# The pointwise product of a convolution branch moves into a recurrent scan, as filler

## The chip, the cores and the metric

The kernel runs on one core of a Trainium2 chip. The time is device microseconds of one execution, start to end, median of several runs. A core has a matrix engine (PE in the profile, whose weight loads are shown apart as PEld), a vector engine (DVE), a scalar engine (ACT), a general engine (POOL), and a queue of commands of its own for each; SP only issues DMAs. Engines run their own instructions in order, and wait for one another through semaphores.

## The reference, cut to what matters

One encoder layer over 1024 positions and 1024 features, all in float32. A combined projection feeds two mixers and two gates; the mixers' outputs are merged, projected, and followed by a feed-forward block.

```python
h = _rmsnorm(x, attn_norm_w)
proj = einsum("bsd,de->bse", h, w_in)             # 1024 -> 8192
glu_in, q, v, z_f, z_b, og, g_a, g_b = split(proj)
a = glu(glu_in)                                   # 512 channels
a = _dwconv_centred(a, dw_w, dw_b)                # 31 taps
a = silu(_layernorm(a, ln_w, ln_b))               # over the 512 channels
a = einsum("bsc,cd->bsd", a, pw_w)                # pointwise product, 512 -> 1024
o = _bi_hgrn2(q, v, z_f, z_b, lb[0], lb[1])       # two gated linear scans, 8 heads of 128
of = rmsnorm_per_head(o) * norm_w
b = einsum("bse,ed->bsd", of * silu(og), o_w)
y = sigmoid(g_a) * a + sigmoid(g_b) * b
x = x + y @ w_out
x = x + (silu(_dwconv3(h2 @ W_gate)) * (h2 @ W_up)) @ W_down,  h2 = _rmsnorm(x)
return _rmsnorm(x, final_norm_w)
```

Of the scan, only what the order of work depends on is needed here: it goes head by head; for each head and each half of the positions the scores inside chunks of 64 are built up by levels (blocks of 8, 16, 32, 64), each level scaling the queries and keys of the next by decays.

## The kernel before, in words

Everything is kept transposed: features in the 128 partitions, positions along the free axis, in two halves of 512. A product of float32 operands is made from three matmuls: `split` (L123) cuts an operand into a high part (a cast on ACT) and a low part (a subtraction on DVE), and `mm3` (L147 to L149) adds high by high, high by low and low by high into one PSUM bank. One such triple is a 128x128 weight block by 512 positions.

The order of PE's instructions is the order in which the program writes them. On the other engines a scheduler orders the instructions, by when it reckons that each can start and by the order in the program.

**Jobs, pieces and streams.** A dense product is a job with two steps: `prep` loads a column block of 128 weights and splits it, `run` issues the matmuls and the evacuation and yields between pieces. A piece of a plain job (`std_job`) is two triples, 6 matmuls; a job over 1024 input features and both halves has 8 pieces, one over 512 features 4. `duo_job` runs two plain jobs side by side, half by half. `pair_job` makes two column blocks with seven products instead of eight block products (a Strassen scheme), with sums of weights and of results made on DVE, ACT and POOL; it has 14 pieces. `run_jobs` strings jobs together, and prepares the next job's weights ahead of its run. A `Stream` hands out pieces: `fill(n)` issues n more of them, fractions being carried over. So a stream of dense work can be laid between the instructions of something else: this is called filler below. `later(n, do)` puts off an action for n pieces.

**Stages.** (1) Up to 84 us: the norm, and the GLU's columns of the projection. (2) 84 to about 430 us: 17 pair jobs make 34 columns of the projection. Beside them `conv_steps` does the depthwise convolution on DVE: 4 channel groups by 31 taps, each tap one operation over 1024 positions (`acc`, L955). After each tap `CONV_FILL` pieces of the pairs are issued. A finished channel group goes to a DRAM scratch, `d_cv`. (3) For each half, the four groups are loaded back (`cx`), summed (`total`, L967), normalised and put through silu, with `LN_FILL` and `LN_LAST` pieces between; their split parts stay in the pages `ch`. (4) The pointwise product: eight plain jobs for each half, over 512 features (4 blocks), with weights `conv_pw_w`, put into the same list as the pairs that are left; results go to the scratch `d_a`. It ends at about 503 us. (5) The scan, until 880 us. `scan_inputs` loads q and the two forget gates (`zi`, L1063) two halves ahead; `Base` makes decays and keys (`Kh`, L1045) and the scores inside blocks of 8 (L1174); `scan_levels` goes through four levels. On each level PE multiplies (`sc`, `ob`: L1162 and L1188), and then DVE scales the keys kG and queries qF by the decays (`tt`, L1042), which the next level's product reads. `scan_states` makes the states of the chunks (transposes `tr`, L1245, and products, L1254) and `outputs` the results of a head (L1295, transposes L1321), stored as `d_bm`. After each level and each step of the states, seven places in a half, stands

```python
def between(fill):
    dense.fill(fill)
    if ahead is not None:
        ahead.step(BASE_STEPS)
    pending.fill(1)
```

where `dense` is the stream of the 22 columns of the projection that the pairs left (the last two as a `duo_job`), `ahead` the next half's `Base`, and `pending` the outputs of the head before. 21 pieces are issued before the first half, `FILL` at each place, and the pieces that are left in the tail, between the outputs of the last head. (6) From 930 us the product with `hgrn_o_w`, whose evacuation `merge` loads `d_a` and the gates; then `w_out` and the feed-forward block, with the same plain and pair jobs.

The activations of the projection stay on chip for half 0 and for a part of half 1; the first blocks of half 1 are loaded and split again for the scan's filler (`h12`, in pages `hx`, of which there are 32, given out in turn). The pages `hx` are also what the results of the scan are loaded into (`bm_loads`).

Of the kernel before, what the change touches and what calls it, by code (L numbers as in the profile page):

```python
# [10 lines left out]
F32 = mybir.dt.float32  # L11
# [5 lines left out]
AX = mybir.AxisListType  # L17

P = 128
FILL = 1.3  # L20
CONV_FILL = 1.6
NPAIRS = 17
LN_FILL = 6
LN_LAST = 12
# [22 lines left out]
def tile_hybrid_encoder(  # L47
# [22 lines left out]
    nc = tc.nc  # L70
    PSUM = bass.MemoryType.PSUM
    V, A, G, T = nc.vector, nc.scalar, nc.gpsimd, nc.tensor

    S, D = x.shape[1], x.shape[2]
    ND = D // P
    CW = conv_dw_w.shape[2]
    CK = conv_dw_w.shape[1]
    NCW = CW // P
# [14 lines left out]
    def nm(s):  # L93
        uid[0] += 1
        return f"{s}_{uid[0]}"
# [3 lines left out]
    def bank(tag):  # L99
        return ps.tile([P, H], F32, tag=tag, name=nm(tag), bufs=BANKS[tag])  # L100

    def page(pool, tag, bufs, dt=F32):
        return pool.tile([P, H], dt, tag=tag, name=nm(tag), bufs=bufs)

    def tmp():
        return page(mp, "tm", 4)

    def ev():
        return page(mp, "ev", 3)

    def hx():
        return page(mp, "hx", 32, F32R)
# [9 lines left out]
    def split(hi, lo, src, eng, late=False):  # L122
        parts = A.copy(hi, src), eng.tensor_tensor(lo, src, hi.bitcast(F32), op=ALU.subtract)  # L123
        if late:
            for i in parts:
                pin(i)
        return hi, lo

    def w_cols(w, r0, nk, c0, cols=P):
        return w[0, r0 : r0 + nk * P, c0 : c0 + cols].rearrange("(k p) e -> p k e", p=P)  # L130

    def raw_w(src, nk):
        t = mp.tile([P, nk, P], F32, tag="wr", name=nm("wr"), bufs=2)
        nc.sync.dma_start(t, src)
        return t

    def w_page(nk, pool=None):
        if pool is None:
            return mp.tile([P, nk, P], F32R, tag="wp", name=nm("wp"), bufs=4)
        return pool.tile([P, nk, P], F32R, tag="wq", name=nm("wq"), bufs=3)  # L140

    def mm3(acc, w, act, k, first, last, again=False):


        whi, wlo = w
        ahi, alo = act
        T.matmul(acc, whi[:, k, :], ahi, start=first, stop=False, skip_group_check=again)  # L147
        T.matmul(acc, whi[:, k, :], alo, start=False, stop=False, skip_group_check=again)  # L148
        T.matmul(acc, wlo[:, k, :], ahi, start=False, stop=last, skip_group_check=again)  # L149
# [7 lines left out]
    def later(n, do):  # L157

        chores.append([n, do])

    def advance_chores(n=1):
        for c in list(chores):
            c[0] -= n
            if c[0] <= 0:
                chores.remove(c)
                c[1]()
# [26 lines left out]
    def run_jobs(jobs, lead=0, prime=0, first=None):  # L193


        live = collections.deque(maxlen=3)

        jobs = jobs if isinstance(jobs, collections.deque) else collections.deque(jobs)
        ready = collections.deque()

        def prepare(n):
            while jobs and len(ready) < n:
                prep, run = jobs.popleft()
                ready.append((run, prep()))
                live.append(ready[-1][1])

        def tick():
            for w in live:
                if isinstance(w, Weights):
                    w.tick()  # L210
            advance_chores()

        prepare(max(prime, 1))
        if prime:
            yield
        while ready:
# [32 lines left out]
    def std_job(src, nk, acts, evac, halves=(0, 1), step=2):  # L249


        def prep():
            raw = raw_w(src, nk)
            return split(w_page(nk), w_page(nk), raw, V)

        def run(w, halves=halves):
            for half in halves:
                acc = bank("mm")
                for k in range(nk):
                    mm3(acc, w, acts(k, half), k, k == 0, k == nk - 1)  # L260
                    if k % step == step - 1 or k == nk - 1:
                        yield
                evac(half, acc)

        return prep, run

    def duo_job(src0, src1, nk, acts, evac0, evac1):

        both = [std_job(src0, nk, acts, evac0), std_job(src1, nk, acts, evac1)]

        def prep():
            return [p() for p, _ in both]

        def run(w):
            for half in range(2):
                for (_, r), wi in zip(both, w):
                    yield from r(wi, (half,))

        return prep, run
# [197 lines left out]
    def scratch(name, *dims):  # L477
        if not dims:
            return dp.tile([P, H], F32, name=name)
        return [scratch(f"{name}_{i}", *dims[1:]) for i in range(dims[0])]  # L480

    d_h = scratch("d_h", ND, 2)
    d_cv = scratch("d_cv", NCW, 2)
    d_a = scratch("d_a", ND, 2)
    d_ga = scratch("d_ga", ND, 2)
    d_gb = scratch("d_gb", ND, 2)
# [12 lines left out]
    def in_cols(c0):  # L499
        return w_cols(w_in, 0, ND, c0)  # L500
# [212 lines left out]
    def store(dst, func=None):  # L713
        def evac(half, x0, x1=None, op=None):
            t = ev()
            if x1 is not None:
                V.tensor_tensor(t, x0, x1, op=op)  # L717
                x0 = t
            if func is not None:
                A.activation(t, x0, func)  # L720
            elif x1 is None:
                A.copy(t, x0)
            nc.sync.dma_start(dst[half], t)

        return evac
# [214 lines left out]
    jobs = collections.deque(in_pair(n) for n in range(1, NPAIRS))  # L940
# [21 lines left out]
    for _ in conv_steps():  # L962
        s_pairs.fill(CONV_FILL)

# [4 lines left out]
            V.tensor_tensor(o, o, t, op=ALU.add)  # L969
        return o  # L970

    pw_jobs = []
    for half in range(2):
        xs = []
        for j in range(NCW):
            if j % 2 == 0:
                both = p1.tile([P, 2, H], F32, tag="ca", name=nm("cx"), bufs=2)
            nc.sync.dma_start(both[:, j % 2, :], d_cv[j][half])
            xs.append(both[:, j % 2, :])
        s_pairs.fill(LN_FILL)  # L980
        mean = bank("ob")
        T.matmul(mean, ones_m, total(xs, tmp()), start=True, stop=True)
        for t in xs:
            V.scalar_tensor_tensor(t, mean, -1.0 / CW, t, op0=ALU.mult, op1=ALU.add)
        s_pairs.fill(LN_FILL)
        sqs = [tmp() for _ in xs]
        for sq, t in zip(sqs, xs):
            A.activation(sq, t, AF.Square)
        rstd = rstd_over_partitions(total(sqs, sqs[0]), CW, "ob", tmp())
        next(rstd)  # L990
        s_pairs.fill(5)
        rs = next(rstd)
        ca = []
        for j, xn in enumerate(xs):
            V.tensor_tensor(xn, xn, rs, op=ALU.mult)
            V.tensor_scalar(xn, xn, vec("lnw", j), vec("lnb", j), op0=ALU.mult, op1=ALU.add)
            A.activation(xn, xn, AF.Silu)
            both = gp0.tile([P, 2, H], F32R, tag="gl", name=nm("ch"), bufs=NCW)
            ca.append(split(both[:, 0, :], both[:, 1, :], xn, V))
        s_pairs.fill(LN_LAST)  # L1000
        at = 0
        while at < len(jobs) and jobs[at] in pw_jobs:
            at += 1
        for i in range(ND):
            job = std_job(
                w_cols(conv_pw_w, 0, NCW, i * P), NCW, lambda k, hf, ca=ca: ca[k], store(d_a[i]), (half,)
            )
            pw_jobs.append(job)
            jobs.insert(at + i, job)
    s_pairs.drain()  # L1010
    Stream(run_jobs(jobs)).drain()
    p1.release()
    gp0.release()

# [1 line left out]
    rest = todo[2 * NPAIRS :]  # L1016
    rest_jobs = [std_job(in_cols(c), ND, h_std, e) for c, e in rest[:-2]]
    (c0, e0), (c1, e1) = rest[-2:]
    rest_jobs.append(duo_job(in_cols(c0), in_cols(c1), ND, h_std, e0, e1))

    h12.clear()
    for k in range(NK2):
# [2 lines left out]
    dense = Stream(run_jobs(rest_jobs))  # L1025
# [343 lines left out]
    for h in range(NH):  # L1369
# [4 lines left out]
        for half in range(2):  # L1374
            i = 2 * h + half
# [12 lines left out]
            for n, _ in enumerate(scan_levels(base, S_t, Tt[:, half])):  # L1388
                if n == 2:
# [4 lines left out]
                    A.copy(v.rearrange("p c e -> p (c e)"), b)  # L1394
                between(FILL)
            qF, kG = base[0], base[1]
            for _ in scan_states(i, kG, v, Tt, Sf, Sb):
                between(FILL)
            kept.append((S_t, v, qF))
            cur = ahead  # L1400
        pending = Stream(outputs(h, kept, Tt, Sf, Sb))

    left = 8 * (len(rest) - 2) + 16 - dense.count
    pending.fill(1)
    dense.fill(left - 20)
    pending.fill(1)
# [209 lines left out]
    gs, jobs = [], []  # L1616
# [183 lines left out]
```

## Time and profile before

| | |
|---|---|
| median of 3 runs | 1791.35 us (1791.15 to 1793.52) |
| span of the profiled execution | 1788.8 us |
| busy PE | 1733.0 us, 97% |
| busy DVE | 1250.4 us, 70% |
| busy ACT | 775.0 us, 43% |
| busy POOL | 153.8 us, 9% |
| moved by DMA | 276.41 MB, mean 155 GB/s |
| HBM read, written | 185.73 MB, 72.61 MB |

The profiled execution is one of its own; the profile gives its span, from the first instruction to the last, and no time from outside, so that its own time is its span and what the device needs around it.

How rows are read: a group of instructions has its line, engine, operation, its output and inputs by the program's names, the number of them, their busy time in us, the mean of one in ns, and the idle time of the engine just before them with what ended it. A row of the waits reads: engine, tile and line that waited, engine, tile and line that released it, us in total, how many, the longest. A row of the timeline reads: start in us, duration, engine, line, operation, and in brackets the idle time before it and its releaser. In a table of stretches each engine has its busy us and, in brackets, its instructions; PEclk is the TensorE clock that was granted, 1 being full speed.

### The profile page before, as it was taken

The page shows a single profiled execution, that of the slowest core. Times are in us where ns is not written, and L with a number is a line of the kernel's source. Part 1 is how long each engine was busy: PE and PEld are TensorE (multiplying, and loading weights), DVE is VectorE, ACT ScalarE, POOL GpSimd, SP SyncE. Part 2 cuts the span into 40 slices and gives each one's busy share as a digit, 9 for nine tenths or more (in the row PEclk, how much of TensorE's full clock was granted, in tenths as well). Part 3 has the DMA queues.
Part 4 walks back from the last instruction along what each step waited for, and adds up shares of the span by engine and source line. Part 5 has one row for each costly group of instructions (what it writes and reads, how often), then busy time and mean ns, then how long its engine had stood idle before and what let it go on. Part 6 is the DMA issues. An engine that isn't in the chain of part 4 may idle for free.

```text
span 1788.8 us, 27583 instructions
## 1 busy us (share of the span) xinstructions
PE 1733.0 (97%) x10632; PEld 1416.7 (79%) x10638; DVE 1250.4 (70%) x1884; ACT 775.0 (43%) x1490; POOL 153.8 (9%) x168
## 2 busy tenths in 40 slices
PE   8989999999999999999999999999999999999997
PEld 6878877888777777777778888878888888888885
DVE  5599999746569999999645557667667667544455
ACT  7344333334555566655442245344344344422123
POOL 2201111000000000000000002011111111000000
PEclk9999999999999999999999999999999999999999
DMA  8657887743663433333257665567667665534233
GB/s 285 216 151 187 185 185 185 199 150 126 199 214 101 125 119 119 119 119 101 90 180 219 200 201 177 153 142 159 151 144 158 142 151 133 161 103 126 79 91 135
DMA packets 317705, 276.41 MB, mean 155 GB/s; under 512 B 14462, under 2 KB 242566, under 8 KB 317574
## 3 DMA queue, kind: packets, MB, share of 16 engines
q1 hardware_dynamic: 276406, 242.15, 43.1%
q0 software_dynamic: 41168, 32.51, 12.6%
q8 instruction: 83, 1.36, 0.3%
q14 instruction: 48, 0.39, 0.1%
HBM read 185.73 MB, written 72.61 MB: 144 GB/s over the span
## 4 chain that ended last, share of the span: by engine, by line
PE 65%; DVE 19%; DMA 5%; issue 4%; ACT 4%; POOL 1%; SPq 0%; POOLq 0%; DVEq 0%; ACTq 0%
PE mm L147 16%; PE mm L148 16%; PE mm L149 16%; PE sc L147 3%; PE sc L149 3%; PE sc L148 3%; DVE acc L955 2%; DVE kG L1042 2%; DVE DE L1042 2%; DVE qF L1042 2%; DVE wp L123 2%; PE tr L147 1%; PE tr L149 1%; PE tr L148 1%; DVE DE L1098 1%
## 5 line engine op out<-in xcount | busy, mean ns | idle before, releaser
L147 PE MATMUL mm<-hx,wp 128*128 128x512 f32 x1128 | 454.8, 403 | 9.8 <-DVE ev L717 4.3
L149 PE MATMUL mm<-hx,wp 128*128 128x512 f32 x1128 | 441.7, 392 | 1.9 <-DVE wp L123 1.9
L148 PE MATMUL mm<-hx,wp 128*128 128x512 f32 x1128 | 441.4, 391 | 0.0
L123 ACT CAST wp<-wr 128x1024 fp32r<-128x1024 f32 (+2 forms) x179 | 167.0, 934 | 359.6 <-PE mm L148 271.5
L147 PEld LDWEIGHTS mm<-hx,wp 128*128 128x128 f32 x1128 | 212.5, 188 | 55.7 <-DVE ev L717 6.7
L123 DVE TENSOR_TENSOR wp<-wr,wp 128x1024 fp32r<-128x1024 f32 (+2 forms) x177 | 191.4, 1082 | 90.4 <-ACT wp L123 90.1
L149 PEld LDWEIGHTS mm<-hx,wp 128*128 128x128 f32 x1128 | 212.6, 188 | 49.3 <-DVE wp L123 3.2
L148 PEld LDWEIGHTS mm<-hx,wp 128*128 128x128 f32 x1128 | 212.9, 189 | 40.4 <-issue 0.2
L955 DVE SCALAR_TENSOR_TENSOR acc<-gl,v_b,acc 128x1024 f32<-128x1024 f32 x120 | 149.0, 1277 | 0.5
L1651 DVE TENSOR_TENSOR xr<-mm,xr 128x512 f32<-128x512 f32 x48 | 33.2, 691 | 73.1 <-PE mm L149 73.1
L367 ACT COPY su<-mm 128x512 f32<-128x512 f32 x78 | 45.2, 579 | 62.5 <-PE mm L149 61.5
L123 ACT CAST wq<-sw 128x1024 fp32r<-128x1024 f32 x39 | 41.0, 1051 | 64.4 <-issue 28.6
L1500 DVE SCALAR_TENSOR_TENSOR tm<-gp,v_a,tm 128x512 f32<-128x512 f32 x88 | 65.9, 749 | 2.0
L147 PE MATMUL mm<-hy,wp 128*128 128x512 f32 x156 | 61.5, 394 | 1.4 <-ACT su L367 1.4
L148 PE MATMUL mm<-hy,wp 128*128 128x512 f32 x156 | 61.1, 392 | 0.0
L147 PE MATMUL sc<-hy,wq 128*128 128x512 f32 x156 | 61.1, 392 | 0.0
L149 PE MATMUL sc<-hy,wq 128*128 128x512 f32 x156 | 61.1, 391 | 0.0
L147 PE MATMUL tr<-hx,wp 128*128 128x512 f32 x156 | 60.8, 390 | 0.0
L149 PE MATMUL tr<-hx,wp 128*128 128x512 f32 x156 | 60.7, 389 | 0.0
L148 PE MATMUL tr<-hx,wp 128*128 128x512 f32 x156 | 60.7, 389 | 0.0
L148 PE MATMUL sc<-hy,wq 128*128 128x512 f32 x156 | 60.7, 389 | 0.0
L149 PE MATMUL mm<-hy,wp 128*128 128x512 f32 x156 | 60.6, 389 | 0.0
(368 smaller groups left out, 3467.6 us busy)
## 6 DMA issues: line engine op xcount, KB each, us to landing
wr<-in_w_in_dram SPq DMA_DIRECT2D x56, 512.0 KB, 4.7
wr<-in_ffn_w_up_dram SPq DMA_DIRECT2D x24, 512.0 KB, 4.9
sw<-in_ffn_w_up_dram SPq DMA_DIRECT2D x44, 256.0 KB, 3.0
d_g<-ft SPq DMA_DIRECT2D x44, 256.0 KB, 2.7
sw<-in_ffn_w_up_dram POOLq DMA_DIRECT2D x20, 512.0 KB, 8.3
sw<-in_w_in_dram SPq DMA_DIRECT2D x34, 256.0 KB, 3.2
d_z<-ev SPq DMA_DIRECT2D x32, 256.0 KB, 3.1
zi<-d_z SPq DMA_DIRECT2D x32, 256.0 KB, 3.2
```

Of the source, the lines that this page charges most:

```text
L123: parts = A.copy(hi, src), eng.tensor_tensor(lo, src, hi.bitcast(F32), op=ALU.subtract)
L147: T.matmul(acc, whi[:, k, :], ahi, start=first, stop=False, skip_group_check=again)
L148: T.matmul(acc, whi[:, k, :], alo, start=False, stop=False, skip_group_check=again)
L149: T.matmul(acc, wlo[:, k, :], ahi, start=False, stop=last, skip_group_check=again)
L367: A.copy(t, acc)
L955: V.scalar_tensor_tensor(acc, g[:, k : k + S], tap(k), acc, op0=ALU.mult, op1=ALU.add)
L1042: V.tensor_tensor(o, a, b, op=op)
L1098: V.reciprocal(ed(D, 7), ed(0, D + 7))
L1500: V.scalar_tensor_tensor(c, g[:, o + k : o + k + H], vec("fdw", k * NF + j), c, op0=ALU.mult, op1=ALU.add,)
L1651: V.tensor_tensor(xr[i][half], acc, xr[i][half], op=ALU.add)
```

## The change

It touches constants and the two places where the pointwise product is made.

- `FILL`, the pieces per place of the scan, goes from 1.3 to 1.58, and `CONV_FILL`, the pieces per tap of the convolution, from 1.6 to 1.4.
- The pointwise jobs are no longer put into the list of pairs. After the layer norm, the split parts of each channel group and half are stored to a new DRAM scratch, `d_ca`: 16 stores of 256 KB. The scan follows the layer norm directly, once the pairs are drained.
- The pointwise product is appended to the filler of the scan, behind the 22 columns: six plain jobs and a duo job, each over both halves, instead of eight jobs for each half. Its matmuls are the same, 192.
- The parts are loaded from `d_ca` into 16 pages `hx`. The loads are put off with `later(8, ...)`: the wait starts when the first pointwise job is prepared, and they are issued eight pieces on, in the middle of the duo job ahead of it. The pages that they take are pages of `h` that the duo job reads last.
- The number of pieces left for the tail is worked out from the longer list.

```diff
-FILL = 1.3
-CONV_FILL = 1.6
+FILL = 1.58
+CONV_FILL = 1.4
...
+    d_ca = scratch("d_ca", NCW, 2, 2)
...
-    pw_jobs = []
     for half in range(2):
...
-        ca = []
         for j, xn in enumerate(xs):
...
             both = gp0.tile([P, 2, H], F32R, tag="gl", name=nm("ch"), bufs=NCW)
-            ca.append(split(both[:, 0, :], both[:, 1, :], xn, V))
+            for dst, part in zip(d_ca[j][half], split(both[:, 0, :], both[:, 1, :], xn, V)):
+                nc.sync.dma_start(dst, part.bitcast(F32))
         s_pairs.fill(LN_LAST)
-        at = 0
-        while at < len(jobs) and jobs[at] in pw_jobs:
-            at += 1
-        for i in range(ND):
-            job = std_job(
-                w_cols(conv_pw_w, 0, NCW, i * P), NCW, lambda k, hf, ca=ca: ca[k], store(d_a[i]), (half,)
-            )
-            pw_jobs.append(job)
-            jobs.insert(at + i, job)
     s_pairs.drain()
-    Stream(run_jobs(jobs)).drain()
...
     rest_jobs.append(duo_job(in_cols(c0), in_cols(c1), ND, h_std, e0, e1))
+    ca = [[None, None] for _ in range(NCW)]
+
+    def ca_loads(half):
+        for j in range(NCW):
+            parts = hx(), hx()
+            for part, src in zip(parts, d_ca[j][half]):
+                nc.sync.dma_start(part.bitcast(F32), src)
+            ca[j][half] = parts
...
+    def pw_first():
+        prep, run = std_job(pw_col(0), NCW, ca_of, store(d_a[0]))
+
+        def loads():
+            later(8, lambda: [ca_loads(half) for half in range(2)])
+            return prep()
+
+        return loads, run
+
+    rest_jobs.append(pw_first())
+    rest_jobs += [std_job(pw_col(i), NCW, ca_of, store(d_a[i])) for i in range(1, ND - 2)]
+    rest_jobs.append(
+        duo_job(pw_col(ND - 2), pw_col(ND - 1), NCW, ca_of, store(d_a[ND - 2]), store(d_a[ND - 1]))
+    )
...
-    left = 8 * (len(rest) - 2) + 16 - dense.count
+    left = 8 * len(rest) + 4 * ND - dense.count
```

Three places of the order show what moves. Names are tiles with a running number. The first is PE's order in the scan, between two products of a level (`tr` is the last transpose of the head before, L1188 the product that reads qF and kG). Before:

```order
L1392 MATMUL tr_6836<-ident,tm_6686 128x128 x4
L147 MATMUL mm_6751<-hx_916,wp_6275 128x512
L148 MATMUL mm_6751<-hx_917,wp_6275 128x512
L149 MATMUL mm_6751<-hx_916,wp_6276 128x512
L147 MATMUL mm_6751<-hx_946,wp_6275 128x512
L148 MATMUL mm_6751<-hx_947,wp_6275 128x512
L149 MATMUL mm_6751<-hx_946,wp_6276 128x512
L1188 MATMUL sc_6814<-qF_6533,kG_6534 64x64 x8
```

and now, in the same place; six more rows like these, with other pages `hx`, stand at the mark, and line numbers are 19 higher in this part:

```order
L1411 MATMUL tr_6628<-ident,tm_6478 128x128 x4
L147 MATMUL mm_6592<-hx_3960,wp_6222 128x512
L148 MATMUL mm_6592<-hx_3961,wp_6222 128x512
L149 MATMUL mm_6592<-hx_3960,wp_6223 128x512
...
L147 MATMUL mm_6592<-hx_905,wp_6222 128x512
L148 MATMUL mm_6592<-hx_906,wp_6222 128x512
L149 MATMUL mm_6592<-hx_905,wp_6223 128x512
L1207 MATMUL sc_6606<-qF_6315,kG_6316 64x64 x8
```

Before, six filler matmuls (a piece) stand ahead of the level's product; now twelve.

The second is DVE's order late in the convolution. `acc` are the taps, of the third and of the last channel group; L967 is the first step of `total` for half 0, which reads the first two channel groups back (`cx`), and so waits for the third group's last tap and a store and a load behind it; `ev` are evacuations of the pairs, and `wp` and `wq` the low parts of their weights. Before:

```order
L123 TENSOR_TENSOR wp_2738<-wr_2731,wp_2737 128x1024
L717 TENSOR_TENSOR ev_2756<-tr_2701,su_2716 128x512
L955 SCALAR_TENSOR_TENSOR acc_2928<-gl_359,v_b,acc_2928 128x1024
L967 TENSOR_TENSOR tm_3497<-cx_3420 128x512
L955 SCALAR_TENSOR_TENSOR acc_2928<-gl_359,v_b,acc_2928 128x1024 x3
L717 TENSOR_TENSOR ev_2803<-su_2788,mm_2700 128x512
```

and now, up to the same evacuation of the same pair:

```order
L968 TENSOR_TENSOR tm_3272<-cx_3222 128x512
L956 SCALAR_TENSOR_TENSOR acc_2760<-gl_375,v_b,acc_2760 128x1024
L718 TENSOR_TENSOR ev_2787<-tr_2728,su_2744 128x512
L123 TENSOR_TENSOR wp_2769<-wr_2762,wp_2768 128x1024
L956 SCALAR_TENSOR_TENSOR acc_2760<-gl_375,v_b,acc_2760 128x1024 x5
L123 TENSOR_TENSOR wq_2777<-sw_2764,wq_2776 128x1024
L718 TENSOR_TENSOR ev_2834<-su_2819,mm_2727 128x512
```

The pair's evacuation in the last row (`ev`, from `su` and `mm`) now comes after 115 taps of the convolution instead of 112.

The third is SP's queue, late in the scan, where there is nothing like it before; `d_bm` are stores of the scan's results, and the five rows between them the first of the 16 loads of the parked parts:

```order
L1346 DMA d_bm_0_273<-ev_8434 128x512
L1016 DMA hx_8616<-d_ca_0_0_119 128x512
L1016 DMA hx_8617<-d_ca_0_1_120 128x512
L1016 DMA hx_8620<-d_ca_0_0_123 128x512
L1016 DMA hx_8621<-d_ca_0_1_124 128x512
L1016 DMA hx_8624<-d_ca_0_0_127 128x512
L1346 DMA d_bm_1_274<-ev_8540 128x512
```

The first five loads stand between two stores of results; the pages that they fill were pages of `h`.

More of the change, by code (lines that the diff above doesn't have):

```diff
@@ L1019, in tile_hybrid_encoder, with pw_col, ca_of @@
     rest_jobs.append(duo_job(in_cols(c0), in_cols(c1), ND, h_std, e0, e1))
+    ca = [[None, None] for _ in range(NCW)]
[5 more added lines that the diff above has]
+            ca[j][half] = parts
+    def pw_col(i):
+        return w_cols(conv_pw_w, 0, NCW, i * P)
+    def ca_of(k, half):
+        return ca[k][half]
+    def pw_first():
[9 more added lines that the diff above has]
+    )
     h12.clear()
```

## The prediction

> **What bounds the kernel now.** First the page's head: the busy times and the shares of the chain that ended last.
>
> ```profile
> span 1788.8 us, 27583 instructions
> PE 1733.0 (97%) x10632; PEld 1416.7 (79%) x10638; DVE 1250.4 (70%) x1884; ACT 775.0 (43%) x1490; POOL 153.8 (9%) x168
> PE 65%; DVE 19%; DMA 5%; issue 4%; ACT 4%; POOL 1%; SPq 0%; POOLq 0%; DVEq 0%; ACTq 0%
> ```
>
> PE is the bound: all but 55.8 us of the span is busy. The change removes no matmul, so it can only win or lose idle time of PE. Where that idle time lies is read from busy times by stage: the pairs beside the depthwise convolution (84 to 340), the pairs alone, the layer norm with the pointwise product (430 to 515), the scan (515 to 880), its tail, and for comparison a full stretch of the merge.
>
> ```profile
> core 0: us, PE busy (x) PEld busy (x) DVE busy (x) ACT busy (x) POOL busy (x), PEclk, DMA share, GB/s
> 84.00:340.00 256.00, 246.81 (x1070) 200.72 (x1069) 242.40 (x258) 98.43 (x139) 37.52 (x38) 0.99 0.77 182
> 340.00:430.00 90.00, 90.00 (x399) 73.94 (x398) 51.99 (x68) 35.80 (x53) 2.11 (x2) 1.00 0.48 148
> 430.00:515.00 85.00, 84.10 (x365) 67.45 (x364) 38.15 (x59) 43.60 (x77) 2.52 (x6) 1.00 0.64 207
> 515.00:880.00 365.00, 346.51 (x4450) 283.51 (x4455) 333.24 (x677) 209.91 (x514) 13.72 (x14) 1.00 0.36 113
> 880.00:960.00 80.00, 75.27 (x409) 61.97 (x408) 38.45 (x61) 31.52 (x68) 3.44 (x3) 1.00 0.62 188
> ```
>
> Read three things. In the pairs alone 399 instructions fill 90.00 us: one 512-column matmul costs 0.226 us. In 430 to 515 PE idles 0.9 us of 85 while DVE has 46.9 us free. In the scan PE idles 18.5 us and DVE is busy 333.24 of 365, 91%: there DVE is nearly the second bound. PE's waits in the scan:
>
> ```profile
> PE ob L1162 <- DVE qF L1042: 6.0, 7, 1.5
> PE tr L1245 <- DVE kG L1042: 4.9, 7, 1.8
> PE sc L1188 <- DVE qF L1042: 3.2, 6, 1.2
> PE ob L1295 <- DVE D L1230: 1.1, 1, 1.1
> PE sc L1254 <- ACT kT L1247: 0.9, 2, 0.5
> PE ob L1162 <- ACT wp L123: 0.9, 1, 0.9
> PE sc L1188 <- issue: 0.2, 1, 0.2
> ```
>
> Together 17.2 us in 25 waits, none over 1.8 us; 15.2 us of it is PE waiting for DVE. That is the stock the change draws on.
>
> **The change, part by part.**
>
> *The pointwise product leaves its stage.* It is 3 x 64 matmuls there.
>
> ```profile
> L147 PE MATMUL mm<-ch,wp x64: 387/392/800, 452.6 to 499.9; 128*128 128x512 f32 x64
> PE mm L147 <- ACT ch L123: 0.6, 1, 0.6
> PE mm L148 <- DVE ch L123: 0.2, 1, 0.2
> ```
>
> 192 x 0.226 = 43.4 us of PE leave it and come back in the scan: nothing won. Only the two waits for its operand go: -0.8 us. Eight loads and splits of weights fewer (each job now does both halves) lie off PE's path: nothing.
>
> *The scan gets more pieces per place.* In the place shown with the change, twelve filler matmuls instead of six stand ahead of the product that waits for qF. Counted over the order, 73 of 105 filler stretches of the scan hold 6 matmuls and 32 hold 12; now 44 and 61. A half of a head gets 996/15 = 66.4 filler matmuls instead of 822/15 = 54.8: 11.6 x 0.226 = 2.6 us more. How long a half lasts is read from the first product of each:
>
> ```profile
> L1174 PE MATMUL sc<-Qh,Kh x1024: 196/196/218, 529.3 to 876.6; 128*32 128x32 f32 x171
> ```
>
> 347.3/15 = 23.1 us, of which DVE works 91%, 21.1. The new half is 23.1 + 2.6 less what goes of the waits (17.2/16 = 1.1): 24.6 to 25.7, and DVE's share falls to at most 86%. Bounds: 29 of the 73 short stretches become long, by 1.36 us, nearly the longest wait; if only the waits behind those go, 29/73 x 17.2 = 6.8 us. If DVE's new slack of 3.5 us a half removes all, 17.2. Between them I take the middle, **-12.0**: an engine that is ahead in one place stays ahead in the next, but the chain of product, kG, qF, next product keeps its length in the 44 places that stay short.
>
> *The convolution's own filler falls from 1.6 to 1.4.* PE executes nothing of that loop but the pairs, so the number only moves DVE's order. In the second place shown with the change, by the evacuation in the last row 115 taps are done instead of 112; the lead of three taps arises in the third to fifth pair and stays. The rows that price it:
>
> ```profile
> PE mm L147 <- DVE ev L717: 4.3, 5, 3.1
> L955 DVE SCALAR_TENSOR_TENSOR acc<-gl,v_b,acc 128x1024 f32<-128x1024 f32 x120 | 149.0, 1277 | 0.5
> L123 DVE TENSOR_TENSOR wp<-wr,wp 128x1024 fp32r<-128x1024 f32 x28 | 34.1, 1218 | 5.6 <-ACT wp L123 5.6
> L717 DVE TENSOR_TENSOR ev<-su,mm 128x512 f32<-128x512 f32 x11 | 7.4, 677 | 0.0
> 305.63 0.69 DVE L967 TENSOR_TENSOR tm<-cx 128x512 f32<-128x512 f32 x1 [3.15 <-DMA cx<-d_cv]
> 310.81 0.71 PE L147 MATMUL mm<-hx,wp 128*128 128x512 f32 x1 [3.12 <-DVE ev L717]
> 312.17 0.63 PE L147 MATMUL mm<-hx,wp 128*128 128x512 f32 x1
> 313.45 0.63 PE L147 MATMUL mm<-hx,wp 128*128 128x512 f32 x1
> 314.56 0.40 PE L147 MATMUL mm<-hx,wp 128*128 128x512 f32 x1
> 315.26 0.39 PE L147 MATMUL mm<-hx,wp 128*128 128x512 f32 x1
> 300.00:320.00 20.00, 16.88 (x67) 13.46 (x67) 16.71 (x17) 4.55 (x7) 3.33 (x3) 0.91 0.77 181
> ```
>
> Three taps are 3 x 1.277 = 3.8 us by which the pairs' DVE work comes later, and since PE waited for an evacuation in five places already, most of it becomes PE waiting: +3.8 at most, 0 at least. Against it: the one long wait, 3.1 us, was DVE's own 3.15 us for a load (cx). By the order its sum now stands six taps, two weight splits and three half-size operations behind the last tap of its channel (12.1 us of DVE work) instead of five taps, two splits and one (9.5), though the load has also moved behind three loads of weights in SP's queue. That wait shrinks by 0 to 2.6, and with it goes the slow spell behind it: triples of matmuls 1.36, 1.28 and 1.11 us apart where 0.68 is normal, 1.7 us in all. Ends +3.8 and -4.3; I take **0**, with the smaller waits spread.
>
> The clock is where a page bears on it. Row: after 3.12 us idle the stretch's granted clock is 0.91. The Trainium skill, "TensorE: Matmul & The Clock Gate", section on what is actually happening, says an idle window of about 3.4 us halves the clock until about as long a window has been busy. By that rule waits of 1 to 2 us cost nothing more, and the term stays 0; by the row alone a wait of just 3 us already costs 1.7, and one such wait left would make the sum 1.7 worse.
>
> *From the layer norm straight to the scan.* The 43.4 us that covered the scan's first loads are gone; the cover left is the rest of the last pair and the 21 pieces ahead of the scan. By the order, the first zi load now waits for the sixth product of the last pair; 139 matmuls, 31.4 us, stand between that and the scan's first product. The chain it must cover, as it ran before:
>
> ```profile
> 503.36 0.92 SPq L1063 DMA_DIRECT2D zi<-d_z  x2
> 522.05 0.76 DVE L1045 SCALAR_TENSOR_TENSOR Kh<-k,kscale,DE 128x512 f32<-128x512 f32 x1
> ```
>
> 19.5 us from the issue to the second Kh. About 12 us of slack: 0.
>
> *Parking.* 16 stores and 16 loads of 256 KB, 24 entries more on SP's queue after eight weight loads less. The stores stand in the layer norm, ahead of the second half's cx loads, with DVE far from busy: 0 to +1. The loads stand where the last in-projection runs (the third place shown with the change). Each waits until PE has read the half-0 pages of h that it overwrites, so SP stops there; queued behind are stores of gates and prefetched pointwise weights. PE uses the first page about one half, 23 us, after the first load may go, and the last some 30 us after. 4.2 MB at 285 GB/s (the page's busiest slice, below) less the scan's 113 take 24 us. I take +0.5, ends 0 and +3.
>
> ```profile
> GB/s 285 216 151 187 185 185 185 199 150 126 199 214 101 125 119 119 119 119 101 90 180 219 200 201 177 153 142 159 151 144 158 142 151 133 161 103 126 79 91 135
> cx<-d_cv SPq DMA_DIRECT2D x8, 256.0 KB, 3.6
> PE tr L1321 <- ACT tm L1314: 2.1, 1, 2.1
> ```
>
> *Tail.* The transpose in the last row finds 18 filler matmuls ahead of it instead of 12, 1.36 us, but a weight cast now stands before it on ACT: -0.7, ends 0 and -1.4.
>
> **Sum.** -0.8 - 12.0 + 0 + 0 + 0.5 - 0.7 = -13.0. The profiled execution spans 1788.8 us; the median of the runs, 1791.35, lies 2.55 above it, which I take for what lies around the span. 1775.8 + 2.55 = **1778** us. All good ends: -0.8 - 17.2 - 4.3 - 1.4 = -23.7, 1767.
>
> **Rivals.**
> 1. *The waits stay.* The chains, not DVE's load, make them: for it speaks that none is longer than 1.8 us and that 44 places keep one piece; against it DVE's 91%. With 0 to 6.8 us won the time is 1783 to 1790.
> 2. *DVE becomes the bound of the convolution.* A pair there costs DVE 11 x 1.277 + 3 x 1.22 + 4 x 0.68 (operations of half the size) = 20.4 us against 84 x 0.226 = 19.0 of PE; a lead from before the loop has hidden the 1.4. If the lead is gone from the start, ten pairs pay 1.4, 14 us: 1792. Against it: only 4.3 us of such waits now.
> 3. *The parked loads come late* (the slower side). Place: PE's first pointwise matmul. If the 16 loads go one after the other at 3.6 us, the landing of cx, they take 58 us where 30 are there, and PE stands 28: 1806. It decides from 43 us on, 2.7 us a load. Against it: 113 GB/s in the scan is 2.3 us per 256 KB already, beside other loads.
>
> **Chances.** Forecast 0.60 (its own range 1770 to 1785); first rival 0.17; second 0.13; third 0.06; the rest unnamed. About 0.2% (3.6 us) is what a measurement of this kernel can tell from no change: faster below 1787.8. The forecast and two thirds of the first rival are faster, some of the rest too: 0.72; the second rival straddles: same 0.13, slower 0.15. Leaving out the third rival and the tails, the range is 1767 to 1793.
>
> **What would show it.** Right: waits of PE for qF and kG in the scan at 3 to 8 us in total, the first-product rows 24.7 to 25 us apart per half, the scan starting some 43 us earlier, DVE's share there at 86%. Wrong: those waits still over 10 us; waits for ev L718 over 8 us, or PEclk below 0.9, between 84 and 340; a wait of PE for the DMA of hx from d_ca; a gap of several us ahead of the first L1193.

## The result, and where the time went

The changed kernel takes 1795.37 us, median of 12 runs (1790.70 to 1801.97). The kernel before, in 12 runs beside and ahead of them, takes 1793.68 (1791.15 to 1800.54). The ratio is 1.001, 95% interval 0.9995 to 1.0025: no change that can be told, where 13 us less had been forecast. The profiled execution is a long one, 1798.91 us with a span of 1797.1; it is set against the 1788.8 of the one before, so 8.3 us have to be found. The medians lie only 1.7 us apart: what follows is the account of two executions, of which the later one is 3.5 us longer than its median.

The head of the page of the changed kernel:

```profile
span 1797.1 us, 27612 instructions
PE 1740.8 (97%) x10638; PEld 1421.5 (79%) x10638; DVE 1250.6 (70%) x1876; ACT 770.3 (43%) x1482; POOL 154.1 (9%) x168
PE 65%; DVE 15%; DMA 9%; issue 6%; ACT 4%; POOL 1%; SPq 0%; POOLq 0%; ACTq 0%; DVEq 0%
```

Then busy times by stage: the convolution, the layer norm with the last pairs, the scan from its first product to its last, the tail.

```profile
84.00:340.00 256.00, 242.81 (x1042) 196.61 (x1042) 241.63 (x257) 96.61 (x135) 37.52 (x38) 0.99 0.75 177
340.00:475.00 135.00, 126.80 (x536) 102.61 (x535) 76.31 (x104) 54.25 (x85) 4.52 (x8) 0.95 0.55 179
503.00:879.00 376.00, 368.74 (x4522) 302.39 (x4521) 324.56 (x650) 209.62 (x515) 14.16 (x14) 1.00 0.39 122
879.00:930.00 51.00, 46.34 (x322) 37.31 (x311) 21.28 (x40) 27.29 (x65) 1.83 (x2) 1.00 0.52 163
```

and the same two last stages of the kernel before, cut at its own scan:

```profile
529.00:877.00 348.00, 329.51 (x4344) 269.61 (x4348) 316.98 (x647) 201.19 (x499) 13.72 (x14) 1.00 0.35 111
877.00:930.00 53.00, 48.27 (x324) 39.50 (x321) 21.59 (x41) 24.00 (x59) 1.83 (x2) 1.00 0.46 147
```

*The scan did what was forecast.* PE idles 7.3 us of it (376 - 368.74), where it idled 18.5. DVE's share fell from 91% to 324.56/376 = 86%. The first products of the halves run from

```profile
L1193 PE MATMUL sc<-Qh,Kh x1024: 196/196/218, 503.1 to 878.7; 128*32 128x32 f32 x171
```

375.6/15 = 25.0 us a half. What is left of the waits there:

```profile
PE ob L1314 <- DVE tb L1061: 2.6, 3, 1.2
PE tr L1264 <- DVE kG L1061: 1.3, 3, 0.5
PE sc L1273 <- ACT kT L1266: 1.2, 3, 0.7
PE sc L1207 <- DVE qF L1061: 1.0, 2, 0.6
PE ob L1181 <- DVE qF L1061: 0.6, 2, 0.3
```

6.7 us instead of 17.2. The tail did not move: 4.7 us idle of it in both.

*The loss lies ahead of the scan.* The 126 matmuls of the 21 pieces ahead of the scan take 28.5 us, so the pairs end at 503.1 - 28.5 = 474.6. In the kernel before they end, with the pointwise product's 43.4 us taken out, at 529.3 - 28.5 - 43.4 = 457.4. That is 17.2 us. 6.3 of them are there at 340 us (28 matmuls fewer by then), 10.9 arise in the layer norm, where the kernel before had no wait of PE at all between 340 and 430. The balance of the two executions: +6.3 convolution, +10.9 layer norm, -11.2 scan, 0 tail, and a rest of +2.3, which was not traced to a stage: 8.3.

PE's waits between 84 and 340 and between 340 and 475, one row each, and the two of the layer norm by themselves:

```profile
PE mm L147 <- DVE ev L718: 8.2, 4, 3.4
...
PE mm L147 <- DVE ev L718: 8.2, 2, 4.5
...
401.83 0.79 PE L147 MATMUL mm<-hx,wp 128*128 128x512 f32 x1 [3.72 <-DVE ev L718]
...
450.08 0.79 PE L147 MATMUL mm<-hx,wp 128*128 128x512 f32 x1 [4.48 <-DVE ev L718]
```

What DVE did ahead of the first of these two:

```profile
393.32 1.29 DVE L994 TENSOR_TENSOR cx<-cx,tm 128x512 f32<-128x512 f32 x2 [2.13 <-ACT tm L520]
394.53 1.00 DVE L995 TENSOR_SCALAR cx<-cx,v_a 128x512 f32<-128x512 f32 x2
395.44 1.29 DVE L994 TENSOR_TENSOR cx<-cx,tm 128x512 f32<-128x512 f32 x2
396.65 0.54 DVE L995 TENSOR_SCALAR cx<-cx,v_a 128x512 f32<-128x512 f32 x1
397.10 1.22 DVE L123 TENSOR_TENSOR wq<-sw,wq 128x1024 fp32r<-128x1024 f32 x1
398.24 1.28 DVE L123 TENSOR_TENSOR ch<-cx,ch 128x512 fp32r<-128x512 f32 x2
399.44 0.68 DVE L123 TENSOR_TENSOR wq<-w,wq 128x512 fp32r<-128x512 f32 x1
400.05 0.68 DVE L123 TENSOR_TENSOR ch<-cx,ch 128x512 fp32r<-128x512 f32 x1
400.65 0.54 DVE L995 TENSOR_SCALAR cx<-cx,v_a 128x512 f32<-128x512 f32 x1
401.10 0.68 DVE L718 TENSOR_TENSOR ev<-su,mm 128x512 f32<-128x512 f32 x1
401.70 0.68 DVE L718 TENSOR_TENSOR ev<-sc,su 128x512 f32<-128x512 f32 x1
```

Nearly the whole block of normalisation, four groups of `cx` and three of their splits, stands here, with two splits of a pair's weights (`wq`, 1.9 us) among it: 7.8 us, and the pair's two evacuations only behind it. PE wanted the bank of the first of them at 398.1 and got it at 401.8.

### The profile page after: what moved, and what is told of

Same layout as the page of the kernel before. It is cut to its first block, busy times and chain, and to the rows that moved or that the text cites. A ratio compares the mean times of both kernels' runs of the same rounds, so it can differ in the third digit from the quotient of the medians.

```text
span 1797.1 us, 27612 instructions
## 1 busy us (share of the span) xinstructions
PE 1740.8 (97%) x10638; PEld 1421.5 (79%) x10638; DVE 1250.6 (70%) x1876; ACT 770.3 (43%) x1482; POOL 154.1 (9%) x168
## 4 chain that ended last, share of the span: by engine, by line
PE 65%; DVE 15%; DMA 9%; issue 6%; ACT 4%; POOL 1%; SPq 0%; POOLq 0%; ACTq 0%; DVEq 0%
PE mm L147 16%; PE mm L149 16%; PE mm L148 16%; PE sc L147 3%; PE sc L149 3%; PE sc L148 3%; DVE acc L956 3%; DMA wr<-wr 2%; DVE wp L123 2%; DMA wr<-sw 2%; DVE DE L1061 2%; DMA sw<-in_ffn_w_up_dram 1%; DVE qF L1061 1%; PE ob L1314 1%; PE tr L147 1%
## 5 line engine op out<-in xcount | busy, mean ns | idle before, releaser
L147 PE MATMUL mm<-hx,wp 128*128 128x512 f32 x1192 | 483.6, 406 | 23.5 <-DVE ev L718 16.4
L149 PE MATMUL mm<-hx,wp 128*128 128x512 f32 x1192 | 469.7, 394 | 2.2 <-DVE wp L123 2.1
L148 PE MATMUL mm<-hx,wp 128*128 128x512 f32 x1192 | 468.9, 393 | 0.0
L123 ACT CAST wp<-wr 128x1024 fp32r<-128x1024 f32 (+2 forms) x171 | 161.9, 948 | 363.0 <-PE mm L148 240.0
L147 PEld LDWEIGHTS mm<-hx,wp 128*128 128x128 f32 x1192 | 226.4, 190 | 74.7 <-DVE ev L718 19.9
L149 PEld LDWEIGHTS mm<-hx,wp 128*128 128x128 f32 x1192 | 226.0, 190 | 54.2 <-DVE wp L123 5.0
L148 PEld LDWEIGHTS mm<-hx,wp 128*128 128x128 f32 x1192 | 226.6, 190 | 43.7 <-issue 0.5
L123 DVE TENSOR_TENSOR wp<-wr,wp 128x1024 fp32r<-128x1024 f32 (+2 forms) x169 | 185.5, 1098 | 107.6 <-ACT wp L123 107.0
```

## The experiments

Each ran beside the kernel before on the same chip; the ratio is to that, with its 95% interval, and where two kernels are compared, it is by these ratios, 0.1% being 1.8 us.

### CONV_FILL back at 1.6

```diff
-CONV_FILL = 1.4
+CONV_FILL = 1.6
```

> The changed kernel with CONV_FILL back at 1.6, the other parts kept. In the profile of the changed kernel the pairs end at 474.6 us instead of 457.1 (500.5 less the 43.4 us of the pointwise product): 17.5 us lost before the scan; the scan wins about 11 of them back. Theory A (the number 1.4 does the damage, by the order that it gives to DVE in the convolution and in the layer norm): most of the 17.5 goes, the waits of PE for ev L718 fall from 16.4 to 4-6 us, and the time is 1778 to 1786. Theory B (the missing pointwise product does it: the second half's layer norm has no filler left, 18 pieces short): waits of PE for ob or for the second half's sums appear, 5 to 20 us, and the time is 1790 to 1805.

1795.16 us, ratio 1.0002 (0.9991 to 1.0012): not better than 1.4. The waits of the convolution fell from 8.2 to 4.8 us, as in theory A, but others came, as in theory B:

```profile
458.09 2.07 PE L519 MATMUL ob<-tm,ones_m 128*128 128x512 f32 x2 [3.87 <-ACT tm L518]
...
PE sc L1181 <- ACT A L1179: 3.7, 1, 3.7
...
L1193 PE MATMUL sc<-Qh,Kh x1024: 196/196/218, 493.1 to 875.3; 128*32 128x32 f32 x171
```

17 pairs have 17 x 14 = 238 pieces. With 1.6 the 124 steps of the convolution take 198 of them and the two layer norms want 58 more; 18 are missing, at the second half's sums. In the kernel before, the pointwise jobs filled that place. So 1.4 is not a number that only moves DVE: without the pointwise product the pairs must last through the second layer norm, and 1.4 saves them for it (174 + 58 = 232).

### The layer norm's filler spread over its groups

```diff
             for dst, part in zip(d_ca[j][half], split(both[:, 0, :], both[:, 1, :], xn, V)):
                 nc.sync.dma_start(dst, part.bitcast(F32))
-        s_pairs.fill(LN_LAST)
+            s_pairs.fill(LN_LAST / NCW)
```

> The changed kernel, with the 12 pieces that follow the four channel groups of a half's layer norm issued three after each group. The convolution's order is as in the changed kernel; only the evacuations of the pairs come ahead of a part of the normalisation on DVE. Theory A1 (the loss is two waits of 3.7 and 4.5 us in the layer norm, each with some 2.5 us of slow matmuls behind it, because the pair's evacuation stands behind the whole block of normalisation on DVE): those go, 8 to 13 us less, 1782 to 1788. Theory A2 (the loss is the lead of taps in the convolution): 1793 to 1797, as the changed kernel.

1787.04 us, ratio 0.9952 (0.9935 to 0.9970), against 1.001 of the changed kernel: some 10 us less, as theory A1 has it. DVE, in the place shown above:

```profile
391.40 1.29 DVE L994 TENSOR_TENSOR cx<-cx,tm 128x512 f32<-128x512 f32 x2 [2.13 <-ACT tm L520]
392.62 1.00 DVE L995 TENSOR_SCALAR cx<-cx,v_a 128x512 f32<-128x512 f32 x2
393.53 0.68 DVE L994 TENSOR_TENSOR cx<-cx,tm 128x512 f32<-128x512 f32 x1
394.13 0.68 DVE L718 TENSOR_TENSOR ev<-su,mm 128x512 f32<-128x512 f32 x1
```

The first evacuation comes 2.7 us after the block's start, not 7.8, and PE's waits of 8.2 us between 340 and 475 are 0.6 us. The scan starts at 488.5, so that the pairs end at 460.0 instead of 474.6. The edit changes no work; it only deals the pairs' pieces out between the groups, and with that the order on DVE and on the queues beside it. That the place of the block among the pairs was the larger part of the loss is shown: 13.0 of the 14.6 us are the waits that went (7.6) and the slow matmuls behind the two long ones (5.4). The span of the profiled execution keeps 8.6 of the 14.6 us (1788.5 against 1797.1). Part of the rest went into idle time of PE later on: 8.3 us instead of 7.3 in the scan, 5.5 instead of 4.7 in the tail, 3.0 instead of 1.7 between 1300 and 1500.

### FILL back at 1.3

```diff
-FILL = 1.58
+FILL = 1.3
```

> The changed kernel with FILL back at 1.3; 29 pieces more are left for the tail. If more pieces per place are what took the scan's waits from 17 to 6 us, they come back: waits for qF and kG 13 to 18 us, and 8 to 12 us more than the changed kernel, 1803 to 1807. If the scan's gain has another cause (its later start, or the order of DVE): no change, 1793 to 1797.

1802.23 us, ratio 1.0035 (1.0022 to 1.0047): some 4.5 us more than the changed kernel, where 8 to 12 were expected. The waits came back in full, 14.0 us for qF and kG:

```profile
PE tr L1264 <- DVE kG L1061: 5.7, 8, 1.8
PE ob L1181 <- DVE qF L1061: 5.1, 7, 0.9
PE sc L1207 <- DVE qF L1061: 3.2, 5, 1.3
...
880.00:930.00 50.00, 50.00 (x247) 42.18 (x246) 9.79 (x15) 22.81 (x55) 1.83 (x2) 1.00 0.51 169
```

but with 42 pieces left for the tail PE is busy there throughout (last row), which gave about 5 us back. So more pieces per place do take the scan's waits away, and the pieces have a second customer, the tail.

### The kernel before with CONV_FILL 1.4 alone

```diff
-CONV_FILL = 1.6
+CONV_FILL = 1.4
```

> The kernel before with CONV_FILL 1.4 alone. Theory A: the same waits as in the changed kernel for ev L717 in the convolution and the layer norm, without the scan's gain: 10 to 17 us more than before, 1803 to 1811. Theory B: the pointwise product still stands beside the second layer norm, so no more than the convolution's 3.8 us: 1793 to 1798.

1806.53 us, ratio 1.0053 (1.0033 to 1.0073), 9.5 us more: theory A, just under the lower end of its 10 to 17 us. The convolution's waits for `ev` are 8.0 us, and in the layer norm, with the pointwise product still behind it, there are 5.3:

```profile
PE mm L147 <- DVE ev L717: 5.3, 2, 3.7
...
L1174 PE MATMUL sc<-Qh,Kh x1024: 196/196/218, 539.0 to 884.7; 128*32 128x32 f32 x171
```

In the profiled execution, the shortest of the six (1798.6), the scan starts 9.7 us later than before (539.0 against 529.3) and lasts about as long. So waits in the layer norm need no parking and no scan filler; the rate alone makes 5.3 of the 8.2 us, by where it lets the layer norm fall in the pairs.

### The first layer norm four pieces later

```diff
-        s_pairs.fill(LN_FILL)
+        s_pairs.fill(LN_FILL if half else LN_FILL + 4)
         mean = bank("ob")
```

> The changed kernel with ten pieces instead of six between the first half's loads and its sum, so that both halves' layer norms fall four pieces later in a pair (and four pieces fewer are left behind them). If what costs is where in the pair the block of normalisation falls, the two waits of 3.7 and 4.5 us in the layer norm shrink to under 2 us in all and the time is 1784 to 1790. If the block costs wherever it stands beside a pair, the waits stay at 6 to 9 us and the time is 1793 to 1798.

1788.38 us, ratio 0.9958 (0.9944 to 0.9971). The block of normalisation is about as long as in the changed kernel (in the first half it starts 7.6 us ahead of the evacuation behind it), and PE waits for no evacuation there; what is left is

```profile
PE ob L529 <- DVE tm L970: 2.5, 2, 1.7
```

So it isn't the block by itself that costs, but the point of the pair at which it falls. The kernel before fits this: its first block also starts 6.6 us ahead of an evacuation of a pair (422.1 to 428.8), without a wait of PE, and its second stands beside the pointwise product.

### CONV_FILL 1.5, with the spread filler

```diff
-CONV_FILL = 1.4
+CONV_FILL = 1.5
```

> The changed kernel with the layer norm's filler spread (three pieces after each group, as in the run before: 1787.0) and CONV_FILL 1.5 instead of 1.4. If the wait of 3.3 to 3.5 us at 175 us in the convolution comes from the tap rate, it goes, and the time is 1781 to 1785; the pairs then end six pieces short of the second layer norm, which costs nothing if only its last twelve pieces, on which no matmul waits, are short. If those do count, as they did with 1.6 (a wait of 3.9 for the sums), 1787 to 1792.

1785.47 us, ratio 0.9947 (0.9930 to 0.9964), against 0.9952 without it: not told apart. The wait at 175 us went, and the scan's first products waited about as long (2.5 and 1.1 us).

### FILL 1.5, with the spread filler

```diff
-FILL = 1.58
+FILL = 1.5
```

> The changed kernel with the layer norm's filler spread and FILL 1.5 instead of 1.58: 8 to 9 pieces more are left for the tail. With 1.3 the waits for qF and kG came back (14.5 us) and the tail's waits went (5 us). If the waits grow in proportion to the stretches that are short again, 1.5 brings back about 3 us and the tail gives 3 to 5: 1785 to 1788. If the scan needs the whole of 1.58: 1790 or more.

1777.63 us (1777.01 to 1778.89), ratio 0.9899 (0.9885 to 0.9913): the fastest of all, and 9.5 us better than the spread alone, far more than expected. The scan and the tail of this kernel, then of the one with the spread and 1.58:

```profile
490.00:852.00 362.00, 355.43 (x4400) 292.42 (x4389) 321.89 (x649) 205.79 (x509) 14.10 (x14) 1.00 0.39 123
852.00:930.00 78.00, 76.82 (x532) 63.41 (x519) 35.91 (x62) 35.67 (x79) 1.83 (x2) 1.00 0.62 205
```

```profile
489.00:865.00 376.00, 367.75 (x4432) 301.39 (x4423) 324.48 (x651) 209.59 (x515) 14.14 (x14) 1.00 0.39 122
865.00:930.00 65.00, 59.53 (x442) 48.32 (x429) 29.05 (x52) 30.88 (x71) 1.83 (x2) 1.00 0.59 192
```

PE idles 6.6 us of the scan instead of 8.3: with eight pieces fewer the waits for qF and kG grew by 2 us, from 4.1 to 6.1, about as expected, but the waits for `tb` and `kT`, 3.9 us with 1.58, are gone. In the tail it idles 1.2 us instead of 5.5. The rule for the tail starts with `dense.fill(left - 20)`; with 1.58 there are 208 - 21 - 176 = 11 pieces left (one more than the expectations of the runs below say), the stream is then owed -9, and the first places of the tail get nothing. The same holds for the kernel before (10 pieces, 4.7 us idle). The two profiled executions lie 12.3 us apart. Tail and scan make 6.0 of that; between 1300 and 1500, which no edit touches, PE did 24 matmuls fewer with 1.58 (850 against 874, some 5 us), 2.8 us of it in two waits for ACT's copies `su` that the kernel with 1.5 doesn't have. Why those waits come and go stays open.

### FILL 1.5 alone, and all three

The first of these is the changed kernel with

```diff
-FILL = 1.58
+FILL = 1.5
```

> The changed kernel with FILL 1.5 and nothing else: the layer norm's two waits (8 us and some 5 of slow matmuls) stay, the tail gets its filler (19 pieces are left for it instead of 10; the rule that deals them out starts 10 below nothing with 1.58, and 1 below with 1.5). With the spread, 1.5 instead of 1.58 was worth 9.4 us (1787.0 to 1777.6). If the two effects add up, 1784 to 1788. If 1.5 only helps where the layer norm has been mended: 1792 to 1796.

1790.56 us, ratio 0.9978 (0.9966 to 0.9990): some 6 us better than the changed kernel, where it gave 9.5 with the spread (the intervals are too wide to tell these two apart); the layer norm's waits stay at 8.2 us. Between the two kernels with FILL 1.5, the spread is worth 14 us (0.9978 to 0.9899).

The second has the spread filler, FILL 1.5 and

```diff
-CONV_FILL = 1.4
+CONV_FILL = 1.5
```

> The changed kernel with all three: the layer norm's filler spread, FILL 1.5, CONV_FILL 1.5. With the spread alone CONV_FILL 1.5 was worth 1.6 us (1787.0 to 1785.5, hardly resolved), since the wait of 3.5 us at 175 us went and two waits of the scan's first products (2.5 and 1.1) came. If these add up: 1775 to 1778. If the shorter pairs beside the second layer norm cost more: 1779 or more.

1779.41 us, ratio 0.9920 (0.9900 to 0.9939): no better than with 1.4. Against the convolution's gain stand two waits of the scan's first products (2.1 and 1.2 us).

### The tail's pieces dealt out otherwise

```diff
-    dense.fill(left - 20)
+    dense.fill(max(left - 20, 0))
```

with the spread filler and FILL 1.58.

> The run with spread filler and FILL 1.58 (1787.0), with the first fill of the tail taken as at least zero, so that the 10 pieces that are left go to the first three places of the tail instead of the last two. With FILL 1.5 instead, 9.4 us were won: PE idles 0.7 us of 880 to 930 instead of 5.5, 2.8 us less of waits in the scan, and a few us later. If the tail's first places were bare and that is what costs, 1781 to 1784. If the pieces are only too few, and the waits move to the last places of the tail: 1786 to 1789.

1788.81 us, ratio 0.9958 (0.9943 to 0.9974): no gain. The pieces now stand at the first places, and the waits went to the last ones:

```profile
900.00:930.00 30.00, 26.64 (x108) 20.38 (x107) 14.91 (x22) 17.60 (x39) 1.83 (x2) 0.89 0.75 240
```

So the pieces are too few for the tail, rather than in the wrong place; FILL 1.5 gives it eight more.

### Parking: 16 stores in the kernel before, and 16 more in the fastest

```diff
             ca.append(split(both[:, 0, :], both[:, 1, :], xn, V))
+            for dst, part in zip(d_ca[j][half], ca[-1]):
+                nc.sync.dma_start(dst, part.bitcast(F32))
```

> The kernel before with only the 16 stores of the parked parts added in the layer norm, nothing reads them. If the stores cost what was taken for them, 0 to 1 us: 1793 to 1797, the same as the kernel before on this chip. If they hold up SP's queue and so the loads behind them (cx of the second half, the weights): 3 us or more, over 1798.

1801.44 us, ratio 1.0032 (1.0021 to 1.0043): 6 us for stores that nothing reads. On SP's queue, and on PE:

```profile
476.87 5.26 SPq L1002 DMA_DIRECT2D d_ca<-ch  x8
...
488.20 0.50 PE L147 MATMUL mm<-ch,wp 128*128 128x512 f32 x1 [3.64 <-ACT wp L123]
```

From the first to the last of eight issues 5.3 us pass on SP (a single one takes 0.32 to 0.74 us). The loads of the pointwise weights stand behind them: the next is issued at 483.4 us, in the kernel before at 477.3. PE waits 3.6 us for a weight, with 2.0 us of slow matmuls behind. That makes most of the 6 us; a wait at 311 us, ahead of all the stores, grew as well, from 3.1 to 4.6.

The other starts from the fastest kernel:

```diff
-                nc.sync.dma_start(dst, part.bitcast(F32))
+    d_cb = scratch("d_cb", NCW, 2, 2)
...
+            for to in (d_ca, d_cb):
+                for dst, part in zip(to[j][half], parts):
+                    nc.sync.dma_start(dst, part.bitcast(F32))
```

> The run with spread filler and FILL 1.5 (1777.6), with every parked part stored twice: 16 stores more in the layer norm. In the kernel before, 16 stores cost 6 us, since the loads of the pointwise weights stood behind them on SP's queue. If the cost lies in what is queued behind them, 0 to 1 us here, where no pointwise weights follow: 1777 to 1779. If it lies in the transfers themselves: 1781 to 1785.

1786.03 us, ratio 0.9943 (0.9927 to 0.9958), against 0.9899: 8 us for 16 stores, where 0 to 1 was expected if what is queued behind them matters, on the ground that nothing urgent is. Something is: the weights of the next pair and the loads of the second half, `cx`, on which the second half's sum waits:

```profile
420.32 2.07 PE L983 MATMUL ob<-tm,ones_m 128*128 128x512 f32 x2 [5.78 <-DVE tm L971]
```

With 16 stores this wait is 0.8 us. The run doesn't decide between its two theories: the `cx` loads are issued 2.7 us later (409.5 us against 406.9), but they also take 7.0 us to land instead of 5.9, and between 395 and 405 us the DMA engines' share is 1.04 instead of 0.81. With 16 stores there is no long wait for them in the changed kernel either, so that they cost little there is likely; a run without them was not made. There was little room for more.

## Why the prediction was wrong, point by point

- *The pointwise product leaves its stage (-0.8)*: right; its operand's waits are gone.
- *More pieces per place (-12.0)*: right. PE's idle time in the scan fell by 11.2 us, a half takes 25.0 us (24.7 to 25 forecast), DVE's share is 86%; with FILL alone undone the waits return. That the size is so near is in part luck: the middle between 6.8 and 17.2 was chosen, not derived. What it left out is that the tail lives on the same pieces.
- *The convolution's own filler (0, ends +3.8 and -4.3)*: this is the step that failed, twice. "PE executes nothing of that loop but the pairs, so the number only moves DVE's order" holds for the loop and not for what follows it. The pairs' pieces are a stock, and the number decides at which piece of which pair the layer norm begins. There the block of normalisation met two evacuations of the pairs, 8.2 us of waits and some 5 of slow matmuls behind them, 10.9 us net against the kernel before (which has small losses of its own there), for which the sum had no term. The second layer norm lost its neighbour besides: beside the pointwise product DVE had no results of a pair to make, beside a pair it has (with the rate alone its wait is 1.5 us, here 4.5). The first run shows that 1.6 wouldn't have done either.
- The convolution's own part of that step came out at the bad end and beyond it: 6.3 us by 340. The lead of three taps arose where it was said, and made a new wait of 3.3 us at 175; the long wait at 310, which was to shrink by up to 2.6 us, is 3.4 us at 317. The sign that the prediction named for this, waits for `ev` L718 of over 8 us between 84 and 340, did come: 8.2.
- *From the layer norm straight to the scan (0)*: right for 1.4; with 1.6 and 1.5 the scan's first products do wait, 3.7 and 2.5 us.
- *Parking (+0.5, 0 to +3)*: right for this kernel. No wait of PE for a page of `d_ca` appears; the 16 loads are issued within 11.3 us and a load lands in 5.1 (median). That "DVE far from busy" makes the stores cheap was no reason: elsewhere 16 of them cost 6 and 8 us, and the loads behind them came later.

```profile
L1016 SPq DMA_DIRECT2D hx<-d_ca x16: 319/382/1309, 830.8 to 842.1; - x16
hx<-d_ca SPq DMA_DIRECT2D x16, 256.0 KB, 5.1
```

- *Tail (-0.7)*: 0; its idle time of 4.7 us went only where the tail got more pieces.
- *What lies around the span (2.55)*: it is 1.8 us in the runs (1798.91 against 1797.1), 0.7 less than taken; this changes nothing in the argument.
- *Rivals*: the second gave 1792 for DVE as the bound of the convolution. The time comes near, the mechanism fits only in part: DVE is no more busy there than before (241.63 of 256 us, 242.40 before), it does things in another order, and the larger loss lies in the layer norm, so that the nearness is luck. The parked loads weren't late, and the scan's waits didn't stay.

## What to carry to other kernels

When work that served as filler in one stage is moved to another, count the pieces of each stream through all the stages that draw on it, and look at what comes to stand beside what; a rate that seems local decides where the next stage begins. Where an engine that evacuates for PE also has a long block of other work, look at which evacuation falls behind it: cutting the block with the filler itself was worth 10 to 14 us here, and moving it by four pieces about as much. And where the last pieces of a stream are dealt out by a rule, check what the rule does when few are left.

## What the runs showed of the hardware

Idle gaps of PE of some 3 us had very different prices. Two executions with the same order there and the same wait, the changed kernel and the one with FILL 1.5 alone; the rows are the wait (the first one's is shown above, at 401.83) and the 5 us behind it:

```profile
401.80:406.80 5.00, 4.97 (x12) 3.90 (x13) 1.27 (x2) 0.67 (x2) 0.00 (x0) 0.50 1.05 387
```

```profile
400.61 0.50 PE L147 MATMUL mm<-hx,wp 128*128 128x512 f32 x1 [3.73 <-DVE ev L718]
400.60:405.60 5.00, 4.99 (x22) 4.15 (x23) 2.32 (x3) 2.17 (x4) 0.00 (x0) 1.00 1.05 390
```

After 3.72 us of idle time the granted clock was 0.50 and 12 matmuls started in 5 us; after 3.73 it was 1.00, and 22 did. The loss behind a wait was counted as the time to the 18th matmul that follows, against 0.228 us each, over all the runs up to the scan. Behind the waits of 2.2 to 4.6 us in the pairs and the pointwise product it was 0.1 to 3.0 us, behind those of 1.7 us or less in the convolution 0.1 to 0.2. The length of the wait doesn't order the losses. This one, in the run with FILL 1.3, has the largest behind it, 3.0 us:

```profile
315.99 0.80 PE L147 MATMUL mm<-hx,wp 128*128 128x512 f32 x1 [2.78 <-DVE ev L718]
```

The shortest with a slow spell is 2.24 us long (at 317.4 in the run with the tail dealt out otherwise), with 1.7 us behind it. The Trainium skill, "TensorE: Matmul & The Clock Gate", section on what is actually happening, says that the window of activity by which the clock is set is free-running, so that the moment of a change depends on where in it the work falls. The pair of executions above fits that. The waits of 2.24 and 2.78 us, shorter than the 3.4 that the section gives for an idle window, do not fit its rule that the half rate comes after one such window; here the measurement decides.

The prediction reckoned with such a spell once (1.7 us); the changed kernel had four such waits, with 1.7, 1.7, 2.8 and 2.6 us behind them. How much of the spread of its runs (11 us) this makes was not tried. An estimate: the mean granted clock was 0.988 in its longest execution (1801.97 us) and 0.993 in its shortest (1790.70), and 0.5% of 1795 us are 9 us, so that the clock may make most of it.
